# The order of the first loads of a batched matrix product, with sixteen rows of the weights sent ahead

## The chip, the cores and the metric

The kernel runs on one core of a Trainium2 chip. The metric is the device time of one execution in microseconds (us). The kernel before takes 515.75 us, the median of three runs (515.63 to 515.79).

## The reference

A batched matrix product in float32: 8 x 16 = 128 independent products of a 256x512 matrix with a 512x384 matrix.

```python
def setup_inputs():
    b1, b2, m, k, n = 8, 16, 256, 512, 384
    return {
        "x": np.random.randn(b1, b2, m, k).astype(np.float32),
        "weight": np.random.randn(b1, b2, k, n).astype(np.float32),
    }

def reference(x, weight):
    return np.matmul(x, weight).astype(np.float32)
```

Every byte of x (67.1 MB) and of the weights (100.7 MB) is read once, and every byte of the result (50.3 MB) is written once.

## The kernel before

The 128 products are handled in `NG` = 32 groups of `G` = 4. A group's x is one load of 2 MB: 128 partitions with 16,384 bytes each. A group's weights are 3 MB: 24,576 bytes in each of 128 partitions. They come in one load, or in two halves of 12,288 bytes per partition in the "short" groups, which are the first four and the last two (`is_short`). A group's result is one store of 1.5 MB.

SyncE issues all loads and all stores but one, from one program, in the order in which that is written. `on_sync` (line 314) first writes out the loads of `LAG` = 4 groups, x and then weights for each. A loop over `rounds` follows with the x load of group n+4, the store of group n and the weights of group n+4. The last groups are written out again. There are two buffers for x (`XS`) and two for the weights (`WS`). So the loads of groups 0 and 1 are issued at once. An x load of group 2 or later waits until the x of two groups before has been cast (`x_cast`, line 114). A load of weights waits until the weights of two groups before have been cast (`w_vcast` and `w_acast`, lines 132 and 133). GpSimd issues the store of one late group in three pieces (`store_rest`).

VectorE (`on_vector`, line 338) casts float32 to bf16. It casts the first x (`next_x(0, NG, -1)`), and then for each group the weights, with the next group's x between or behind them. In a short group `cast_short` (line 212) waits for one half of the weights (`h_in`, line 217), casts it in four pieces, and does the same with the second half. In the other groups VectorE casts eleven of the sixteen pieces and ScalarE the last five.

TensorE transposes the cast x into PSUM (`transpose`, line 239), ScalarE copies the transposes to SBUF as bf16 (`evacuate`, line 228), TensorE multiplies (`multiply`, line 254), and ScalarE copies the products to the store's buffer (`copy_out`, line 292). A product of group 0 needs all of that group's weights cast, since `multiply` waits for both counts of casts at its head.

Each transfer adds 16 to a semaphore when it has landed. The halves of the weights use `h_in`, one semaphore for each half of each of the two buffers.

## Time and profile before

| | us |
|---|---|
| median of three runs | 515.75 |
| lowest and highest run | 515.63, 515.79 |
| the profiled execution's own time | 516.01 |
| its span in the profile | 514.2 |

| engine | busy us | share of the span |
|---|---|---|
| PE (TensorE matmul) | 316.8 | 62% |
| PEld (TensorE weight load) | 222.5 | 43% |
| DVE (VectorE) | 397.6 | 77% |
| ACT (ScalarE) | 409.5 | 80% |
| POOL (GpSimd) | 3.7 | 1% |

| transfers | |
|---|---|
| read from HBM, written to HBM | 167.77 MB, 50.33 MB |
| mean rate over the span | 424 GB/s |
| packets | 15686, 218.18 MB |

The profile is of one execution. Times in it count from the start of the span. SPq is SyncE's issuing of transfers, which is not counted as busy time. A digit of the DMA row is the busy share of the 16 DMA engines in one fortieth of the span, in tenths. A row of busy time by stretches gives the stretch, its length, the busy time of each engine with the number of instructions, the granted TensorE clock, the share of the DMA engines and the rate. In these rows a packet is counted in the stretch in which it starts, so a short stretch can show a share above 1. The chain that ended last is followed back from the last instruction, at each step to what released it.

### The profile page before, as it was taken

Reading aid. Unit: us, or ns where it says so; the run is one execution under the profiler, and the core shown is the slowest. Engines: PE = TensorE matmul, PEld = TensorE weight load, DVE = VectorE, ACT = ScalarE, POOL = GpSimd, SP = SyncE. Lnnn points to the kernel's source line nnn. Section 1 sums busy time; section 2 is a strip of 40 time slices with the busy share of each in tenths; the row PEclk is TensorE's granted clock in tenths of the full one; section 3 lists DMA queues with packets and bytes.
Section 4 is the critical chain, followed back from the end, with each engine's and each line's share of the span. In section 5 each row is a group of like instructions: output and inputs, shape, how many; then the busy total and the mean of one; then the engine's idle time right before and its main releaser. Section 6 shows DMA issues by size and latency. Waiting matters only on the chain.

```text
span 514.2 us, 11664 instructions
## 1 busy us (share of the span) xinstructions
PE 316.8 (62%) x4512; PEld 222.5 (43%) x4512; DVE 397.6 (77%) x462; ACT 409.5 (80%) x387; POOL 3.7 (1%) x9
## 2 busy tenths in 40 slices
PE   2277837556675575866568656567545676474782
PEld 2255525434454343544435534345434354353551
DVE  2788757798777887778977779777798777887980
ACT  1365576997898989789978989987998798989752
POOL 0000000000000000000000000000000000010000
PEclk9687785877787778668776868886878787778887
DMA  8999999999999999999999999999999999999997
GB/s 334 429 427 422 438 423 427 436 430 435 420 427 433 433 436 429 425 429 433 440 427 428 427 435 429 438 426 426 431 437 435 425 426 429 435 435 420 422 426 308
DMA packets 15686, 218.18 MB, mean 424 GB/s; under 512 B 1728, under 2 KB 1728, under 8 KB 3008
## 3 DMA queue, kind: packets, MB, share of 16 engines
q1 hardware_dynamic: 15312, 216.54, 98.8%
q0 software_dynamic: 368, 1.57, 0.7%
q8 instruction: 3, 0.05, 0.0%
q14 instruction: 3, 0.02, 0.0%
HBM read 167.77 MB, written 50.33 MB: 424 GB/s over the span
## 4 chain that ended last, share of the span: by engine, by line
DMA 55%; DVE 31%; issue 9%; PE 1%; DVEq 1%; SPq 1%; ACT 0%; POOLq 0%
DMA w_sb<-in_weight_dram 55%; DVE w_bf L207 20%; DVE w_bf L223 5%; DVE x_bf L194 5%; PE po L283 1%; SPq L138 0%; DVEq L360 0%; SPq L121 0%; DVEq L64 0%; DVEq L203 0%; ACT out_sb L300 0%; SPq L133 0%; DVEq L191 0%; DVEq L217 0%; SPq L448 0%
## 5 line engine op out<-in xcount | busy, mean ns | idle before, releaser
L207 DVE CAST w_bf<-w_sb 32x1536 bf16<-32x1536 f32 x286 | 271.9, 951 | 81.9 <-DMA w_sb<-in_weight_dram 70.7
L265 PE MATMUL po<-w_bf,x_t 128*32 128x384 bf16 x3968 | 197.1, 358 | 34.1 <-DVE w_bf L207 29.5
L247 PE MATMUL pt<-identity,x_bf 128*128 128x128 f32 x512 | 114.7, 414 | 153.5 <-DVE x_bf L194 153.5
L207 ACT CAST w_bf<-w_sb 32x1536 bf16<-32x1536 f32 x130 | 190.9, 1468 | 5.5 <-DMA w_sb<-in_weight_dram 2.3
L247 PEld LDWEIGHTS pt<-identity,x_bf 128*128 128x128 f32 x512 | 103.4, 224 | 165.4 <-issue 165.1
L265 PEld LDWEIGHTS po<-w_bf,x_t 128*32 128x32 bf16 x3968 | 116.1, 105 | 113.8 <-issue 53.0
L300 ACT COPY out_sb<-po 128x768 f32 (+1 forms) x128 | 102.5, 801 | 58.8 <-PE po L265 54.7
L234 ACT COPY x_t<-pt 128x1024 bf16<-128x1024 bf16 x128 | 123.6, 1020 | 21.2 <-PE pt L247 20.6
L194 DVE CAST x_bf<-x_sb 128x1024 bf16<-128x1024 f32 x128 | 79.9, 688 | 12.3 <-DMA x_sb<-in_x_dram 11.5
L223 DVE CAST w_bf<-w_sb 64x1536 bf16<-64x1536 f32 x48 | 45.8, 955 | 7.4 <-DMA w_sb<-in_weight_dram 6.0
L234 ACT ACT_TABLE_LOAD x1 | 1.3, 1283 | 10.6 <-PE pt L247 10.6
L174 POOL DMA_DIRECT2D out_dram<-out_sb x3 | 3.1, 1020 | 458.9 <-DMA out_dram<-out_sb 458.9
L283 PE MATMUL po<-w_bf,x_t 128*128 128x384 bf16 x32 | 5.4, 326 | 0.4 <-DVE w_bf L223 0.4
L283 PEld LDWEIGHTS po<-w_bf,x_t 128*128 128x128 bf16 x32 | 3.1, 98 | 2.7 <-issue 0.7
masks.py:199 POOL TENSOR_SCALAR_AFFINE_SELECT identity<-identity 128x128 f32<-128x128 f32 x1 | 0.3, 283 | 0.2 <-POOL identity L306 0.2
L306 POOL MEMSET identity<- 128x128 f32 x1 | 0.2, 204 | 0.5 <-POOLq L64 0.5
L437 POOL MEMSET const-bfloat16-1.0<- 128x1 bf16 x1 | 0.1, 96 | 0.0
L437 POOL MEMSET const-uint8-127<- 128x1 uint8 x1 | 0.1, 96 | 0.0
L437 POOL MEMSET const-float32-0.0<- 128x1 f32 x1 | 0.1, 93 | 0.3 <-issue 0.3
L437 POOL MEMSET const-float32-1.0<- 128x1 f32 x1 | 0.1, 93 | 0.0
## 6 DMA issues: line engine op xcount, KB each, us to landing
w_sb<-in_weight_dram SPq DMA_DIRECT2D x26, 3072.0 KB, 18.1
x_sb<-in_x_dram SPq DMA_DIRECT2D x32, 2048.0 KB, 22.3
out_dram<-out_sb SPq DMA_DIRECT2D x31, 1536.0 KB, 25.0
w_sb<-in_weight_dram SPq DMA_DIRECT2D x12, 1536.0 KB, 16.7
out_dram<-out_sb POOLq DMA_DIRECT2D x1, 1440.0 KB, 16.8
out_dram<-out_sb POOLq DMA_DIRECT2D x1, 60.0 KB, 7.1
out_dram<-out_sb POOLq DMA_DIRECT2D x1, 36.0 KB, 17.6
```

The source lines that it names most:

```text
L174: e.dma_start(out=dram[p : p + k], in_=out_sb[p : p + k, a : a + R], max_dma_last_dim=R // 2 * N * 4,).then_inc(rest_out, 16)
L194: e.tensor_copy(out=x_bf[s % BS][:, rows].rearrange("p r (s q c) -> p r s q c", s=S, c=KO), in_=x_sb[s % XS][:, rows].rearrange("p r (q s ...
L207: copy(out=w_bf[(s * G + i) % WBS][h * C : (h + 1) * C], in_=w_sb[s % WS][i * C : (i + 1) * C, h * KO : (h + 1) * KO, :],).then_inc(w_vcas ...
L223: e.tensor_copy(out=w_bf[(n * G + d * SH + a) % WBS][h * p : (h + 1) * p], in_=w_sb[n % WS][a * p : (a + 1) * p, r : r + KO, :],).then_inc ...
L234: e.copy(out=x_t[s % TS][:, 2 * q : 2 * q + 2], in_=pt[(s * T + q) % PT][:].bitcast(bf16),).then_inc(t_copied, 1)
L247: ins = e.transpose(pt[(s * T + q) % PT][:, rr, h, :], words[:, 2 * q + rr, h :: KO // 2], identity[:],)
L265: ins = e.matmul(po[(s * T + q) % PO][mine, rr, :N], x_t[s % TS][:, 2 * q + rr, ko // 2, mine, ko % 2], w_bf[(s * G + i) % WBS][:, ko, :], ...
L283: ins = e.matmul(po[(s * T + q) % PO][:, rr, :N], x_t[s % TS][:, 2 * q + rr, ko // 2, :, ko % 2], w_bf[(s * G + q) % WBS][:, ko, :], start ...
L300: e.copy(out=out_sb[:, bass.ds(slot(t, U, s) * R + 2 * q, 2), :], in_=po[(s * T + q) % PO][:, :, :N],).then_inc(o_copied, 1)
L306: e.memset(identity[:], 0.0).then_inc(id_done, 1)
L437: nc = _bacc.Bacc("TRN2", target_bir_lowering=False, num_devices=1)
```

## The change

Three things change in the loads of the first group, and nothing in the other groups.

The first half of the first weights is loaded by two transfers instead of one: partitions 0 to 15 (`FIRST` = 16), and then partitions 16 to 127. The first has a semaphore of its own, `w_first`; the second keeps `h_in`. Both together move the same bytes to the same place as the one transfer before.

These two are now issued ahead of the first x load; the second half of the weights is issued behind it. Then the loads of groups 1 to 3 follow as before.

VectorE waits for `w_first` as well, ahead of its first cast of weights. The order of its casts is as before: the first x, then the first half of the weights, then the second.

```diff
+    FIRST = 16
...
+    w_first = sems("w_first", 1)[0]
...
-    def load_w(e, t, U, s):
+    def load_w(e, t, U, s, halves=None):
...
-        for h in range(d):
+        for h in halves or range(d):
             sem = h_in[s % WS * 2 + h] if is_short(n) else w_in[s % WS]
-            e.dma_start(
-                w_sb[s % WS][:, h * k : (h + 1) * k, :],
-                w_rows[bass.ds(n * (G * K) + h * (G // d * K), G // d * K)].rearrange(
-                    "(p k) n -> p k n", k=k
-                ),
-            ).then_inc(sem, 16)
+            dst = w_sb[s % WS][:, h * k : (h + 1) * k, :]
+            src = w_rows[bass.ds(n * (G * K) + h * (G // d * K), G // d * K)].rearrange(
+                "(p k) n -> p k n", k=k
+            )
+            if isinstance(n, int) and n == 0 and h == 0:
+                e.dma_start(dst[:FIRST], src[:FIRST]).then_inc(w_first, 16)
+                dst, src = dst[FIRST:], src[FIRST:]
+            e.dma_start(dst, src).then_inc(sem, 16)
...
             e.wait_ge(h_in[n % WS * 2 + d], turns * 16 + 16)
+            if isinstance(n, int) and n == 0 and d == 0:
+                e.wait_ge(w_first, 16)
...
-        for n in range(LAG):
+        load_w(e, 0, NG, 0, [0])
+        load_x(e, 0, NG, 0)
+        load_w(e, 0, NG, 0, [1])
+        for n in range(1, LAG):
             load_x(e, 0, NG, n)
             load_w(e, 0, NG, n)
```

## The prediction

> **What bounds the kernel now.** I read first the page's head, its DMA rows and the chain that ended last; then busy time by stretches; then the first 30 us in order of time; then the first microseconds in fine stretches.

> ```profile
> span 514.2 us, 11664 instructions
> DMA  8999999999999999999999999999999999999997
> GB/s 334 429 427 422 438 423 427 436 430 435 420 427 433 433 436 429 425 429 433 440 427 428 427 435 429 438 426 426 431 437 435 425 426 429 435 435 420 422 426 308
> q1 hardware_dynamic: 15312, 216.54, 98.8%
> DMA 55%; DVE 31%; issue 9%; PE 1%; DVEq 1%; SPq 1%; ACT 0%; POOLq 0%
> ```

> The DMA engines are at nine tenths in all slices but the first and the last, and SP's queue accounts for 98.8% of their time. VectorE (31% of the chain) stands between two loads, but that alone does not make it the limit: what matters is whether the DMA engines ever ran dry. The stretches answer that. Their columns are stretch, length, busy time of PE, PEld, DVE, ACT and POOL with counts, TensorE clock, DMA share, GB/s.

> ```profile
> 0.00:1.90 1.90, 0.00 (x0) 0.00 (x0) 0.00 (x0) 0.00 (x0) 0.69 (x6) 1.00 0.00 0
> 1.90:4.00 2.10, 0.00 (x0) 0.00 (x0) 0.00 (x0) 0.00 (x0) 0.00 (x0) 1.00 0.96 242
> 4.00:13.00 9.00, 3.44 (x16) 3.27 (x16) 3.09 (x5) 2.36 (x3) 0.00 (x0) 1.00 1.00 428
> 13.00:26.00 13.00, 3.04 (x14) 3.05 (x15) 9.64 (x13) 4.50 (x6) 0.00 (x0) 0.61 1.01 428
> 26.00:39.00 13.00, 9.76 (x160) 6.65 (x162) 10.83 (x13) 7.89 (x10) 0.00 (x0) 0.89 1.01 428
> 100.00:200.00 100.00, 65.06 (x972) 45.45 (x968) 80.38 (x93) 88.82 (x84) 0.00 (x0) 0.78 1.01 430
> 400.00:480.00 80.00, 49.43 (x721) 35.10 (x720) 64.76 (x75) 71.22 (x67) 3.05 (x3) 0.78 1.00 429
> 480.00:506.00 26.00, 20.25 (x305) 13.12 (x304) 18.66 (x22) 14.90 (x18) 0.00 (x0) 0.93 1.01 425
> 506.00:508.00 2.00, 0.00 (x0) 0.00 (x0) 0.00 (x0) 0.00 (x0) 0.00 (x0) 0.86 0.92 381
> 510.00:511.00 1.00, 0.00 (x0) 0.00 (x0) 0.00 (x0) 0.00 (x0) 0.00 (x0) 0.50 0.75 298
> 511.00:512.00 1.00, 0.00 (x0) 0.00 (x0) 0.00 (x0) 0.00 (x0) 0.00 (x0) 0.50 0.27 108
> 512.00:513.00 1.00, 0.00 (x0) 0.00 (x0) 0.00 (x0) 0.00 (x0) 0.00 (x0) 0.50 0.09 33
> ```

> From 4 us to 506 us the share is 1.00 or more and the rate 425 to 430 GB/s, under whatever the other engines do. So the bytes are the bound, and a microsecond that the engines lose or win at the start is carried to the end. Lost at the start now: 1.90 us in which nothing moves, and in 1.90 to 4.00 us 2.10 x 242 GB/s = 0.508 MB, which at 428 GB/s would take 1.19 us, so 0.91 us more. 2.81 us in all. In that second stretch the share is 0.96: the engines are occupied, and yet slow. At the end the engines finish over some 2 us (shares 0.75, 0.27, 0.09), so they are not equally late.

> **The change, part by part.** The first 30 us, in order of time (start, length, engine, line, what; in brackets the idle time before it and what ended it):

> ```profile
> 0.90 0.39 SPq L121 DMA_DIRECT2D x_sb<-in_x_dram  x1
> 1.35 0.89 SPq L138 DMA_DIRECT2D w_sb<-in_weight_dram  x2
> 8.65 2.50 DVE L194 CAST x_bf<-x_sb 128x1024 bf16<-128x1024 f32 x4 [8.65 <-DMA x_sb<-in_x_dram]
> 11.18 0.33 SPq L121 DMA_DIRECT2D x_sb<-in_x_dram  x1
> 12.41 3.91 DVE L223 CAST w_bf<-w_sb 64x1536 bf16<-64x1536 f32 x4 [1.26 <-DMA w_sb<-in_weight_dram]
> 17.22 3.91 DVE L223 CAST w_bf<-w_sb 64x1536 bf16<-64x1536 f32 x4 [0.90 <-DMA w_sb<-in_weight_dram]
> 21.16 0.81 SPq L138 DMA_DIRECT2D w_sb<-in_weight_dram  x2
> 22.13 2.50 DVE L194 CAST x_bf<-x_sb 128x1024 bf16<-128x1024 f32 x4 [0.99 <-DMA x_sb<-in_x_dram]
> 22.96 3.52 PE L247 MATMUL pt<-identity,x_bf 128*128 128x128 f32 x16 [10.07 <-DVE x_bf L194]
> 24.18 2.84 ACT L234 COPY x_t<-pt 128x1024 bf16<-128x1024 bf16 x3 [8.50 <-PE pt L247]
> 24.65 0.33 SPq L121 DMA_DIRECT2D x_sb<-in_x_dram  x1
> 25.91 7.86 DVE L223 CAST w_bf<-w_sb 64x1536 bf16<-64x1536 f32 x8 [1.28 <-DMA w_sb<-in_weight_dram]
> ...
> 37.98 0.36 SPq L160 DMA_DIRECT2D out_dram<-out_sb  x1
> ```

> *The swap.* VectorE's program still casts the first x before any weights. Its x now lies behind 1.57 MB of weights, 3.7 us at 428 GB/s, so the cast starts near 12.4 instead of 8.65, even with no loss at the start. Then the casts run back to back: 2.50 + 3.91 + 3.91 us from 12.4 end at 22.8, where they ended at 21.13. Two issues wait for these casts. The third x load goes from 11.18 to 15.0, the third weights from 21.16 to 22.8. Nothing runs dry: when the weights are issued, 12.58 MB have been issued before them, and 4.36 MB (to 13 us: 0.508 MB and 9 x 428 GB/s) and 9.8 x 428 GB/s = 4.19 MB have moved; 4.0 MB, 9.4 us, still wait. The next x cast goes from 22.13 to 22.8 and ends at 25.3, still before its successor's data (25.91), so VectorE has caught up there. The x load behind it on SP goes from 24.65 to 25.3, and the stores only come after 37 us. TensorE and ScalarE start the second x some 0.7 us later, each with 8.5 us or more of idle time ahead of it now. Cost: nothing, covered by 9.4 us of queued transfers; without that cover it would be 1.6 us.

> *The added wait and issue.* One more wait on VectorE for the first 16 rows, which landed ahead of what it waits for anyway: 0. One more issue on SP ahead of the transfers in the queue: between nothing and 0.39 us of SP's time, after the first transfer has already been handed over. It is covered as long as the engines have work, which is the next point. Both are in straight-line code, not in a loop.

> *An earlier start.* The first issue is at 0.90 us and takes 0.39; the first packet starts 0.61 us after its end.

> ```profile
> DMA packets 15, 0.25 MB, mean 82 GB/s; under 512 B 0, under 2 KB 0, under 8 KB 0
> ```
> ```profile
> DMA packets 31, 0.51 MB, mean 127 GB/s; under 512 B 0, under 2 KB 0, under 8 KB 0
> ```

> (the packets that start by 3.0 us, and by 4.0 us.) A packet is one row of x, 0.25 MB / 15 = 16.4 KB. By 3.0 us not even each of the 16 engines has begun one. From 1.90 to 4.00 us, 31 packets take 2.10 x 16 x 0.96 / 31 = 1.04 us each, where 16.4 KB at 428 / 16 = 26.8 GB/s take 0.61. With 16 rows in the first transfer every engine can have one row at once. At best the issue shrinks with the rows (0.39 x 16/128 = 0.05, gain 0.34) and the thin flow is gone (0.91): -1.25 us. At worst nothing: the engines may be slow in their first packets for a reason that lies with them, as the share of 0.96 suggests. I take -0.4, nearer to nothing because of that share.

> *Sixteen neighbouring rows at once.* This is what no row shows. In every load of before, 16 engines write 128 partitions at 26.8 GB/s each, 8 partitions to an engine. Whether 26.8 GB/s belongs to the engine or to the place that 8 partitions share cannot be seen. If to the engine, the first 16 rows of 12,288 B take 0.46 us side by side: cost 0. If to the place, partitions 0 to 15 lie in as few as 16 / 8 = 2 places, and the transfer takes 16 / 2 x 0.46 = 3.66 us: cost 3.20. If a place's eight partitions come in two runs of four, they lie in 4 places: 1.83 us, cost 1.37, with the other 12 places idle. I take 1.37, the value between the ends. [...]

> *The other 112 rows.* [...] If the engine limits, 7 x 0.46 = 3.2 us and cost 0. If the place does, the 12 places that the first 16 rows left alone hold 8 rows each, 3.66 us: at least 0.46 lost; if the engines met in pairs all along, 3.2. I take 0.6, near the lower end, because the engines are spread over all places and the whole x rows that follow on each engine fill holes.

> Sum against the profiled execution's 516.01 us: -0.4 + 1.37 + 0.6 = +1.57, 517.6. The median of the runs is 515.75, so there 517.3. A measurement of this kernel can tell about 0.2%, 1.03 us, from no change.

> **The rivals.** *No crowding, an earlier start (faster or no change).* The rate belongs to the engine. Then -0.4 remains: 515.35, with ends 515.75 and 514.5. It decides as faster by 0.2% when at least 1.03 of the 1.25 us is won, so when the issue shrinks and the thin flow of 1.90 to 4.00 goes almost wholly. For it: the steady rate is flat at 425 to 430 GB/s, and 31 slow packets lie ahead. Against it: the share of 0.96 there says that work was at hand.

> *An uneven deal (slower).* An engine has 8 rows of a 128-row transfer. If the 16 rows go to two engines, and the 112 to all 16, two engines carry 7 x 0.46 = 3.2 us more to the end: 518.95, less what they were early by (up to 2 us in the last stretches). Or the crowd is two places deep: 3.20 + 0.9 - 0.4 = +3.7, 519.45. Against it: 16 and 112 both divide by 16. [...]

> *Starvation by the later casts (slower).* Priced above at 1.6 us; it needs 9.4 us of queue to vanish. I leave it 1 in 100, within the uneven deal's chance.

> **How the numbers follow.** Crowding (forecast): 0.52; its own range +0.7 to +2.7 us, 516.4 to 518.5 (the first 16 rows at 0.9 to 2.3 and the rest at 0.2 to 0.8); 0.05 of it lies under 516.78. Earlier start without crowding: 0.38, of which 0.15 below 514.72 and 0.23 above. Uneven or deeper: 0.10, of which 0.01 within 1.03 us. Slower 0.47 + 0.09 = 0.56; same 0.05 + 0.23 + 0.01 = 0.29; faster 0.15. The range 514.8 to 518.8 leaves out the lower tail of the earlier start and most of the uneven deal, under 0.2.

> **What would show it.** In the changed kernel's stretches the thin flow of 1.90 to 4.00 lasts to about 6 us, and the total lost before the steady 428 GB/s is 4.4 us instead of 2.8; the first x cast starts near 14 us, not 12.4. Without crowding it starts by 12.1 and the loss is about 2.4. The stretches from 13 us on must keep a share of 1.00, and the cast of the second weights must come as late or early as the first x's landing moved; if the share falls there, the swap was not covered. Uneven dealing would show in the last stretches: a share of 2/16 over some 3 us. I am wrong if the first packets come before 1.6 us and 428 GB/s is reached at once.

## The result and the profile after

The changed kernel takes 517.57 us, the median of six runs (517.33 to 518.08), against 515.73 us before (515.54 to 516.18). The ratio is 1.0037, with a 95% interval of 1.0026 to 1.0047: slower by 1.84 us. The profiled execution took 517.33 us.

The page of the changed kernel:

```profile
span 515.6 us, 11666 instructions
DMA  8999999999999999999999999999999999999997
GB/s 283 420 422 428 439 418 432 432 429 433 431 427 428 436 426 433 426 431 436 440 418 430 430 431 439 437 420 426 431 432 437 436 417 432 432 433 424 423 427 322
q1 hardware_dynamic: 15328, 216.54, 98.9%
DMA 55%; DVE 31%; issue 9%; PE 1%; DVEq 1%; SPq 1%; ACT 0%; POOLq 0%
```

The queue moves the same 216.54 MB, and the chain has the same shares. What differs is the first fortieth: 283 GB/s instead of 334. The stretches of the changed kernel (columns as in the prediction):

```profile
0.00:1.90 1.90, 0.00 (x0) 0.00 (x0) 0.00 (x0) 0.00 (x0) 0.69 (x6) 1.00 0.00 0
1.90:4.00 2.10, 0.00 (x0) 0.00 (x0) 0.00 (x0) 0.00 (x0) 0.00 (x0) 1.00 0.96 205
4.00:6.00 2.00, 0.00 (x0) 0.00 (x0) 0.00 (x0) 0.00 (x0) 0.00 (x0) 1.00 1.04 301
6.00:8.00 2.00, 0.00 (x0) 0.00 (x0) 0.00 (x0) 0.00 (x0) 0.00 (x0) 1.00 1.00 279
8.00:10.00 2.00, 0.00 (x0) 0.00 (x0) 0.00 (x0) 0.00 (x0) 0.00 (x0) 1.00 1.03 385
10.00:13.00 3.00, 0.00 (x0) 0.00 (x0) 0.00 (x0) 0.00 (x0) 0.00 (x0) 1.00 1.01 431
...
0.00:13.00 13.00, 0.00 (x0) 0.00 (x0) 0.00 (x0) 0.00 (x0) 0.69 (x6) 1.00 0.86 281
13.00:26.00 13.00, 4.30 (x19) 3.94 (x20) 11.52 (x15) 5.04 (x5) 0.00 (x0) 1.00 1.00 421
...
400.00:480.00 80.00, 49.26 (x720) 34.88 (x719) 64.49 (x76) 71.21 (x66) 3.02 (x3) 0.78 1.00 429
...
512.00:513.00 1.00, 0.00 (x0) 0.00 (x0) 0.00 (x0) 0.00 (x0) 0.00 (x0) 0.50 0.57 227
513.00:514.00 1.00, 0.00 (x0) 0.00 (x0) 0.00 (x0) 0.00 (x0) 0.00 (x0) 0.50 0.20 79
```

From 1.9 to 10 us the engines are occupied all the time (share 0.96 to 1.04) and move 205 to 385 GB/s, where before they moved 428 from 4 us on. By 13 us they have moved 13 x 281 = 3.65 MB, which is 8.53 us at 428 GB/s, so 4.47 us are lost instead of 2.81: 1.66 us more. In the next 13 us, at 421, 0.2 us more are lost. Both together are 1.87 us, near the 1.84 us between the medians. The two profiled executions themselves lie only 1.32 us apart (517.33 and 516.01), so some 0.5 us of this is not seen at their end; that is as much as runs of the kernel before differ (515.54 to 516.18). Late in the run the rate is what it was.

The first issues and casts of the changed kernel, in order of time:

```profile
0.90 0.40 SPq L146 DMA_DIRECT2D w_sb<-in_weight_dram  x1
1.36 0.40 SPq L148 DMA_DIRECT2D w_sb<-in_weight_dram  x1
...
14.23 2.50 DVE L199 CAST x_bf<-x_sb 128x1024 bf16<-128x1024 f32 x4 [14.23 <-DMA x_sb<-in_x_dram]
...
16.65 7.85 DVE L230 CAST w_bf<-w_sb 64x1536 bf16<-64x1536 f32 x8
...
24.52 0.80 SPq L148 DMA_DIRECT2D w_sb<-in_weight_dram  x2
24.53 2.50 DVE L199 CAST x_bf<-x_sb 128x1024 bf16<-128x1024 f32 x4
...
27.77 7.86 DVE L230 CAST w_bf<-w_sb 64x1536 bf16<-64x1536 f32 x8 [0.74 <-DMA w_sb<-in_weight_dram]
```

The issue of 16 rows takes 0.40 us, as long as that of 112 or of 128. The first x cast comes at 14.23 us. VectorE casts without a pause until 27.03 (24.53 + 2.50), and then waits for data again, so it has caught up. The DMA share over 13 to 26 us is 1.00: the engines did not run dry for it.

### The profile page after: what moved, and what is told of

It is laid out like the page before. It is cut to its first block, busy times and chain, and to the rows that moved or that the text cites. A ratio compares the mean times of both kernels' runs of the same rounds, so it can differ in the third digit from the quotient of the medians.

```text
span 515.6 us, 11666 instructions
## 1 busy us (share of the span) xinstructions
PE 312.6 (61%) x4512; PEld 221.0 (43%) x4512; DVE 397.4 (77%) x462; ACT 409.5 (79%) x387; POOL 3.7 (1%) x9
## 2 busy tenths in 40 slices
DMA  8999999999999999999999999999999999999997
## 3 DMA queue, kind: packets, MB, share of 16 engines
q1 hardware_dynamic: 15328, 216.54, 98.9%
q0 software_dynamic: 368, 1.57, 0.7%
## 4 chain that ended last, share of the span: by engine, by line
DMA 55%; DVE 31%; issue 9%; PE 1%; DVEq 1%; SPq 1%; ACT 0%; POOLq 0%
DMA w_sb<-in_weight_dram 55%; DVE w_bf L212 20%; DVE x_bf L199 5%; DVE w_bf L230 5%; PE po L290 1%; SPq L148 0%; DVEq L370 0%; SPq L124 0%; DVEq L66 0%; DVEq L208 0%; ACT out_sb L307 0%; SPq L136 0%; DVEq L196 0%; SPq L146 0%; DVEq L222 0%
## 5 line engine op out<-in xcount | busy, mean ns | idle before, releaser
L272 PE MATMUL po<-w_bf,x_t 128*32 128x384 bf16 x3968 | 193.3, 353 | 34.8 <-DVE w_bf L212 28.6
L272 PEld LDWEIGHTS po<-w_bf,x_t 128*32 128x32 bf16 x3968 | 114.7, 103 | 111.7 <-issue 49.0
## 6 DMA issues: line engine op xcount, KB each, us to landing
w_sb<-in_weight_dram SPq DMA_DIRECT2D x26, 3072.0 KB, 18.1
```

The source lines that it names most:

```text
L272: ins = e.matmul(po[(s * T + q) % PO][mine, rr, :N], x_t[s % TS][:, 2 * q + rr, ko // 2, mine, ko % 2], w_bf[(s * G + i) % WBS][:, ko, :], ...
```

## The experiments

### The swap alone

(against the kernel before; `load_w` takes the half to be loaded as in the change)

```diff
-        for n in range(LAG):
+        load_w(e, 0, NG, 0, [0])
+        load_x(e, 0, NG, 0)
+        load_w(e, 0, NG, 0, [1])
+        for n in range(1, LAG):
```

> The first half of the first weights goes ahead of the first x in one transfer of 128 rows; nothing is split. Theory (neighbouring rows crowd each other): no change, 515.4 to 516.0 us, ratio 0.999 to 1.001, with the first x cast near 12.2 us and the loss at the start about 2.8 us as before. Rival 1 (the later casts on VectorE cost the time): +1.8 us as in the changed kernel, ratio 1.0035.

Measured: 516.07 us against 515.65, ratio 1.0008 (0.9999 to 1.0017). Stretches and the first x cast of this kernel:

```profile
1.90:4.00 2.10, 0.00 (x0) 0.00 (x0) 0.00 (x0) 0.00 (x0) 0.00 (x0) 1.00 1.05 304
4.00:6.00 2.00, 0.00 (x0) 0.00 (x0) 0.00 (x0) 0.00 (x0) 0.00 (x0) 1.00 0.98 418
```
```profile
11.98 2.50 DVE L194 CAST x_bf<-x_sb 128x1024 bf16<-128x1024 f32 x4 [11.98 <-DMA x_sb<-in_x_dram]
```

The median lies a little above the expected 515.4 to 516.0. The flow is near its full rate from 4 us on (418 GB/s). Rival 1 falls as the cause: of 1.84 us, the swap explains some 0.4, and its interval reaches to no change.

### The split alone

(against the changed kernel)

```diff
-        load_w(e, 0, NG, 0, [0])
-        load_x(e, 0, NG, 0)
-        load_w(e, 0, NG, 0, [1])
-        for n in range(1, LAG):
+        for n in range(LAG):
```

> The first x stays first; the first half of the weights comes in 16 and 112 rows behind it. Theory (crowding): the whole loss stays, +1.4 to +2.2 us, ratio 1.003 to 1.004, and the slow packets come behind the x, between 7 and 14 us. Rival 1 (the swap costs it): no change, ratio 0.999 to 1.001. Rival 2 (16 rows in the cold first packets cost it, not the split as such): less than +0.6 us.

Measured: 518.95 us against 515.65, ratio 1.0064 (1.0050 to 1.0078), +3.3 us. The split costs more in the second place than at the head; the theory had it right that it costs, but its +1.4 to +2.2 us were too small by more than 1 us. Its two rivals, no change and less than +0.6 us, fall. Stretches of this kernel:

```profile
6.00:8.00 2.00, 0.00 (x0) 0.00 (x0) 0.00 (x0) 0.00 (x0) 0.00 (x0) 1.00 1.11 434
8.00:10.00 2.00, 0.00 (x0) 0.00 (x0) 0.00 (x0) 0.00 (x0) 0.00 (x0) 1.00 0.98 166
10.00:13.00 3.00, 1.97 (x10) 2.00 (x11) 2.50 (x4) 0.79 (x1) 0.00 (x0) 1.00 1.02 279
13.00:16.00 3.00, 1.69 (x8) 1.28 (x7) 0.00 (x0) 2.99 (x4) 0.00 (x0) 1.00 0.93 287
```

The x flows at 434 GB/s, and behind it, where the 16 and the 112 rows come, the rate falls to 166 and 279.

### The same bytes ahead, cut by columns

(against the changed kernel)

```diff
-    FIRST = 16
+    FIRST = 1
...
-                e.dma_start(dst[:FIRST], src[:FIRST]).then_inc(w_first, 16)
-                dst, src = dst[FIRST:], src[FIRST:]
+                e.dma_start(dst[:, :FIRST], src[:, :FIRST]).then_inc(w_first, 16)
+                dst, src = dst[:, FIRST:], src[:, FIRST:]
```

> The order of the change, but the small first transfer takes the same 196,608 bytes as one eighth of the columns of all 128 partitions (1,536 bytes in each), and the second the other seven eighths. Theory (crowding of neighbouring rows): no loss, 515.3 to 516.1 us, ratio 0.999 to 1.001. Rival 2 (one more transfer, or a small one at the start, costs it): +1 to +2 us, ratio 1.002 to 1.004.

Measured: 515.81 us against 515.65, ratio 1.0004 (0.9995 to 1.0013). Stretches of this kernel:

```profile
1.90:4.00 2.10, 0.00 (x0) 0.00 (x0) 0.00 (x0) 0.00 (x0) 0.00 (x0) 1.00 0.97 293
4.00:6.00 2.00, 0.00 (x0) 0.00 (x0) 0.00 (x0) 0.00 (x0) 0.00 (x0) 1.00 1.01 419
```

The order of the change, the number of its transfers and the bytes in each are the same, and the loss is gone: 419 GB/s from 4 to 6 us, where the changed kernel has 301. Rival 2 falls. Nothing is won over the kernel before either.

### Sixty-four rows instead of sixteen

(against the changed kernel)

```diff
-    FIRST = 16
+    FIRST = 64
```

> The change with 64 and 64 rows instead of 16 and 112. [...] Rival 2 (an extra transfer costs a fixed time): as the change, +1.8 us. Rival 3 (a small first transfer costs it): less than the change, under +1 us.

Measured: 518.95 us against 515.65, ratio 1.0063 (1.0049 to 1.0077), +3.3 us. Stretches of this kernel:

```profile
4.00:6.00 2.00, 0.00 (x0) 0.00 (x0) 0.00 (x0) 0.00 (x0) 0.00 (x0) 1.00 1.02 215
6.00:8.00 2.00, 0.00 (x0) 0.00 (x0) 0.00 (x0) 0.00 (x0) 0.00 (x0) 1.00 0.96 203
8.00:10.00 2.00, 0.00 (x0) 0.00 (x0) 0.00 (x0) 0.00 (x0) 0.00 (x0) 1.00 0.98 229
10.00:13.00 3.00, 0.00 (x0) 0.00 (x0) 0.00 (x0) 0.00 (x0) 0.00 (x0) 1.00 1.00 426
```

Half the partitions, half the rate: 203 to 229 GB/s from 4 to 10 us with the engines fully occupied (shares 0.96 to 1.02), where the kernel before moves 428. A fixed price of 1.8 us for an extra transfer, or a price for small first transfers alone, would have given less than 3.3 us.

### The price of each piece by itself

Four kernels add loads to the kernel before, behind the first weights, into the store's buffer while it is not in use; ScalarE waits for them ahead of its first copy to it. Their data is used for nothing. The core of the edits:

```diff
+            if n == 0:
+                extra(e)
...
+        # 128 rows of half the length
+        e.dma_start(out_sb[:, : R // 2], src[:, : R // 2]).then_inc(extra_in, 16)
...
+        # 16 neighbouring rows, four times
+        for j in range(4):
+            e.dma_start(out_sb[:16, j * R : (j + 1) * R], src[:16]).then_inc(extra_in, 16)
...
+        # 16 rows, 8 apart, four times
+        for j in range(4):
+            e.dma_start(out_sb[j::8, j * R : (j + 1) * R], src[j::8]).then_inc(extra_in, 16)
...
+        # 112 rows
+        e.dma_start(out_sb[16:, :R], src[16:]).then_inc(extra_in, 16)
```

> The kernel before with one extra load behind the first weights, 128 rows of 6,144 bytes (786 KB), into a buffer that is not in use yet. Both theories: the bytes at 428 GB/s, +1.8 us, 517.6 us.

> The same extra bytes as four loads of 16 neighbouring rows (partitions 0 to 15) of 12,288 bytes. Theory (crowding, four places): four times as long, 7.3 us, so +7 us, 522.8 us (two places: +14.6). If the engine alone limits: +1.8 us as with 128 rows, plus at most 0.4 us for each transfer.

> The same four loads of 16 rows, but of partitions 8 apart (0, 8, 16 and so on to 120). [...] If a transfer of 16 rows as such is slow: the same as with neighbouring rows.

> The kernel before with one extra load of partitions 16 to 127, 12,288 bytes each (1.38 MB). At the engines' full rate 3.2 us. Theory (crowding): 0.9 us more, +4.1 us, 519.8 us. If only the 16 rows crowd: +3.2 us, 518.9 us.

| extra load | MB | median us | against 515.79 | ratio (95% interval) |
|---|---|---|---|---|
| 128 rows of 6,144 bytes | 0.79 | 517.72 | +1.9 | 1.0039 (1.0025 to 1.0054) |
| 4 x 16 neighbouring rows | 0.79 | 523.78 | +8.0 | 1.0154 (1.0137 to 1.0171) |
| 4 x 16 rows, 8 apart | 0.79 | 520.02 | +4.2 | 1.0082 (1.0065 to 1.0099) |
| 112 rows | 1.38 | 521.24 | +5.45 | 1.0106 (1.0089 to 1.0123) |

Stretches of the kernel with four loads of 16 neighbouring rows:

```profile
16.00:18.00 2.00, 0.00 (x0) 0.00 (x0) 0.74 (x2) 0.00 (x0) 0.00 (x0) 0.82 1.24 135
18.00:20.00 2.00, 0.00 (x0) 0.00 (x0) 1.94 (x3) 0.00 (x0) 0.00 (x0) 0.50 1.11 119
20.00:22.00 2.00, 0.00 (x0) 0.00 (x0) 1.58 (x2) 0.00 (x0) 0.00 (x0) 0.50 0.98 119
```

of the one with rows 8 apart:

```profile
16.00:18.00 2.00, 0.00 (x0) 0.00 (x0) 0.73 (x2) 0.00 (x0) 0.00 (x0) 0.75 0.98 197
18.00:20.00 2.00, 0.00 (x0) 0.00 (x0) 1.94 (x3) 0.00 (x0) 0.00 (x0) 0.50 0.95 262
```

and of the one with 112 rows:

```profile
16.00:18.00 2.00, 0.00 (x0) 0.00 (x0) 0.52 (x2) 0.00 (x0) 0.00 (x0) 1.00 0.98 289
18.00:20.00 2.00, 0.00 (x0) 0.00 (x0) 1.94 (x3) 0.00 (x0) 0.00 (x0) 1.00 1.06 248
20.00:22.00 2.00, 0.00 (x0) 0.00 (x0) 1.72 (x2) 0.00 (x0) 0.00 (x0) 1.00 0.93 293
```

The two kernels with 16 rows have the same number of transfers, rows and bytes; only the partitions differ (with the rows of the source that go to them), and the price falls from 8.0 to 4.2 us, the rate from a little over a quarter of 428 GB/s to about a half. Neither the number of rows nor the number of transfers does that. An estimate, with one engine's 428 / 16 = 26.8 GB/s to a place: four places for 16 neighbours (107 GB/s) and eight for rows 8 apart (214) fit; two places (54) don't. 119 to 135 and 197 to 262 GB/s are in the rows here, which hold some other packets as well. The places themselves stand in no record, nor which partitions share one; partitions 8 apart are slowed too, so it is not neighbours alone.

The traces also hold the duration of each packet, one row of a load. In the kernel before, a row of 12,288 bytes takes 0.46 us once the flow is steady. Here the 33 such rows that start from 16.3 to 19.9 us take 1.81 us in the median with neighbouring partitions; with partitions 8 apart, the 41 that start from 15.7 to 18.1 us take 0.92 to 1.08. In the kernel with 64 and 64 rows, the 128 rows take 0.95 in the median. That is about four times and twice 0.46, as it would be with four engines and two engines to a place.

What the runs don't separate is where the rows go from where they come from: other partitions always mean other rows of the weights in HBM. One thing speaks against a crowd on the reading side. In the kernel of the next section with one load of 16 neighbouring rows behind the weights, rows of x that start among and behind these take up to 1.87 us instead of 0.61, though they are read from another array. That points to the writing side; no run shows it by itself.

The 112 rows are the surprise: 1.38 MB is 3.2 us at 428 GB/s, so 2.2 us are crowding, where 0.9 were expected. How their rows are dealt to the engines stands in no record, so no run shows why. The packets show how much: no row of 12,288 bytes that starts from 15.2 to 19.75 us takes more than 1.11 us, where 0.46 is the steady time and 1.81 that of 16 neighbouring rows. The rows of x behind are slowed as well: the slowest takes 1.25 us instead of 0.61.

### What the head hides

Three more kernels ask why the split costs 3.3 us behind the x and the whole change only 1.84: one extra load of 16 neighbouring rows behind the first weights, the same load as the very first transfer, and 112 rows as the very first.

```diff
+        e.dma_start(out_sb[:16, :R], src[:16]).then_inc(extra_in, 16)
...
     def on_sync(e):
         U = 2
+        extra(e)
         for n in range(LAG):
```

> One extra load of 16 neighbouring rows of 12,288 bytes (197 KB) behind the first weights. By the price from the four such loads, (8.0 - 1.9) / 4 = 1.5 us of crowding each, and 0.46 us for the bytes: +2.0 us, 517.8 us.

> The same extra load, but as the very first transfer, ahead of the first x. Theory (the slow first packets and the crowding of these 16 rows lie beside each other): less than behind the weights, +0.4 to +1.2 us, 516.2 to 517.0 us. Rival (the two add up, and the head hides nothing): +2.0 us as behind the weights.

> One extra load of partitions 16 to 127 (1.38 MB) as the very first transfer, which cost +5.45 us behind the first weights. If slow first packets and crowding lie beside each other wherever it crowds: up to 0.8 us less, +4.6 to +5.0 us, 520.4 to 520.8 us. If only the 16 rows hide them: +5.4 us, 521.2 us.

Measured against 515.60: 517.78 us (+2.2; ratio 1.0047, 1.0033 to 1.0060), 516.45 us (+0.85; 1.0016, 1.0006 to 1.0025) and 520.47 us (+4.9; 1.0097, 1.0081 to 1.0112). The head hides 1.35 us of the 16 rows' 2.2, and some 0.6 us of the 112 rows' 5.45, which was measured in another set of runs. Stretches of the kernel with 16 rows at the head:

```profile
1.90:4.00 2.10, 0.00 (x0) 0.00 (x0) 0.00 (x0) 0.00 (x0) 0.00 (x0) 1.00 1.01 218
4.00:6.00 2.00, 0.00 (x0) 0.00 (x0) 0.00 (x0) 0.00 (x0) 0.00 (x0) 1.00 0.92 393
6.00:8.00 2.00, 0.00 (x0) 0.00 (x0) 0.00 (x0) 0.00 (x0) 0.00 (x0) 1.00 1.11 475
```

From 1.90 to 4.00 us it moves 218 GB/s, where before moves 242 there without the extra rows. So the thin flow of the start and the crowding lie beside each other, for 1.35 of the 2.2 us. Why they can is not shown.

## Why the prediction was right

**The time and the sign.** 517.3 us was forecast and 517.57 measured, within the forecast case's own range of 516.4 to 518.5. Crowding of neighbouring rows is the cause: the cut by columns takes the loss away (ratio 1.0004), and which partitions 16 rows go to sets their price (+8.0 us or +4.2 for four loads).

**The swap at nothing.** Right within what can be told: +0.4 us with an interval from none to 0.9. The cover that was named held: VectorE waits for data again at 27 us, and the share stays at 1.00 or more while the weights are issued late.

**The added issue at nothing.** Right: with the cut by columns, which has the same extra issue, the ratio is 1.0004.

**The earlier start, -0.4 us.** Its first half failed: the issue does not shrink with its rows (0.40 us for 16), and nothing moves before 1.90 us. What came in its place is the overlap with the crowding. It was not named, and it is worth 1.35 us for the 16 rows. The swap alone and the cut by columns speed up the flow from 1.90 to 4.00 in their profiles (304 and 293 GB/s against 242), but no run shows a gain in time from it.

**The 16 rows, +1.37 us.** Right as to crowding and its size: (8.0 - 1.9) / 4 = 1.5 us each in a row of four, and 2.2 - 0.46 = 1.7 us for a single one. That 16 neighbouring rows take about four times as long is what the rates (119 to 135 GB/s instead of 428) and the packets (1.81 us instead of 0.46) show. The forecast's four places were an assumption, taken as the value between the ends; no run shows the two runs of four partitions behind it.

**The 112 rows, +0.6 us.** Mis-sized: 2.2 us alone. No run shows how these rows are dealt to the engines. The step that put the value near the lower end, because the engines are spread over all places and the next rows fill the holes, does not hold: the flow is at 248 to 293 GB/s all the while, and the rows that follow are slowed too (up to 1.25 us instead of 0.61) instead of filling holes.

**The sum.** With the measured terms, 1.7 + 2.2 would be 3.9 us for the two pieces, and 3.3 were measured for them behind the x; less 1.35 at the head that makes about 2, against 1.84 measured. The forecast's 1.57 came out near that because errors cancel: the 112 rows were 1.6 us too cheap and the 16 rows 0.3, while the head was about 1 us too dear and the two pieces cost 0.6 less together than apart. The sign and the cause were right; that the time came out within 0.3 us is luck.

**The rivals.** The rival without crowding is ruled out. An uneven deal would have been slow to the end, with a share of 2/16 over some 3 us; from 10 us on the changed kernel runs at 421 to 431 GB/s, and the last two stretches in which anything moves have shares of 0.57 and 0.20. Starvation did not come.

**What was to be seen.** The loss of 4.4 us at the start (4.47) and the cast near 14 us (14.23) were right. The thin flow lasts to about 10 us and not to 6, since the 112 rows spread it.

## What to carry to other kernels

Where transfers are the bound, ask of each which partitions it touches, not only how many bytes it has. Here a load cut by partitions left all 16 engines busy at little more than a quarter of their rate (119 of 428 GB/s) or at half of it (203), and the busy share did not show it; the GB/s beside it did. If a small piece is to go ahead, try to cut it by columns, over all 128 partitions, and measure whether going ahead is worth anything: here it was not.

## What the runs showed that was not expected

- A transfer of 112 neighbouring rows is crowded too: +5.45 us for 1.38 MB, instead of 3.2.
- An issue on SyncE takes 0.40 us for 16 rows, as for 112 or 128. In the kernel with 64 and 64 rows the first three take 0.58 each; why is open.
- 16 crowded rows as the very first transfer cost 0.85 us and behind other loads 2.2. At the head the flow is thin even without them (242 GB/s from 1.90 to 4.00 us); that the two lie beside each other is the likely reading, from these numbers alone.
